# A Mamba layer inside a four-layer trunk: 64-row state tiles, softplus without a reciprocal, two groups projected from unnormed rows, two blocks of the last projection side by side

## The chip, the cores and the metric

The kernel runs on one core of a Trainium2 chip, in one launch. The metric is the device time of a run in microseconds (us). The kernel before took 1758.85, 1759.35 and 1761.85 us in three runs; the median is 1759.35 us.

## The reference

One inference step of four layers: an RG-LRU block, a Mamba-2 block (SSD), an RWKV-7 block and another RG-LRU block, each followed by a squared-ReLU MLP. 256 prompt tokens and 64 sample tokens (8 sequences of 8) go through the same weights, in float32. The change touches the Mamba-2 block alone:

```python
z, xbc, dt = split(rmsnorm(x, w) @ w_in, [2048, 2048 + 4096])
xbc = silu(causal_conv(xbc))                    # width 4, per channel
xs, B, C = split(xbc)                           # 8 groups: 256 x, 128 B, 128 C channels each
dt = softplus(dt + dt_bias)                     # 32 heads, 4 in a group
acs = cumsum(dt * A)                            # in a chunk (128 tokens) or a sample sequence (8)
y = (C B^T * exp(acs_i - acs_j) * mask) (dt * xs) + (C * exp(acs)) s_start
s_fin = s_start * exp(acs_end) + sum_j exp(acs_end - acs_j) dt_j x_j B_j^T   # new state
yg = (y + d_skip * xs) * silu(z)
yg = yg * rsqrt(mean over the group's 256 channels of yg^2)
x  = x + (yg * norm_w) @ w_out
```

Each of the 8 sample sequences has its own 128 x 256 state in every group, and all eight new ones are outputs.

## The kernel before

Features lie on the 128 partitions and the 320 tokens along them. Weights stream from one array in 512 KB chunks; each becomes a rounded half `whi` (an ACT copy, L494) and the rest `wlo` (a DVE subtraction, L495), in three buffers each. The activations are split likewise (`xh`, `xl`), and a product is three matmuls (L498 to L500): high by high, high by low, low by high. A chunk is 24 matmuls of 128x128 weights on 320 columns, called mains below.

The Mamba block (339 to 668 us of the profiled run) begins with the norm's factor `rs` per token. The inputs `xh`, `xl` hold at first the rows without that factor, so that projections start before it is known. `steps` computes dt for all heads on 32 partitions: softplus through `log1p_tail`, a scan `acs`, transposes (L926). `project(g)` computes a group's x half, its B and C and its z (two chunks each), and for each pair of results a convolution (ACT L849, DVE L851). Group 0 is projected from the unnormed rows, and `scaled` (L944, DVE) multiplies each result by `rs` into the tile `zs`, from which ACT copies it (L964, L965). Then `renorm` (L647, DVE; the split on ACT and DVE) makes the normed rows, and groups 1 to 7 use those; ACT copies their results straight from PSUM.

`ssd(g)` transposes x and B (L998), forms C B^T, the decays and masks (`em`), the old states' part (L1040), then the y products (L1072 to L1080), `yg`, and the group's norm (`nacc`, matmuls L595 and L611 to L613, `nrs`), whose result is split into `ygh`, `ygl`. For the new sample states ACT makes eight copies of B, each masked to one sequence (`bx`, L1060). 16 matmuls of 128x128 weights on 256 columns (L1101, L1102: x high, x low) go in four blocks into the bank `st_ps`, and DVE adds each block to the scaled old states (L1103; the scaling is L1095).

`weave` interleaves the parts of `ssd(g)` with those of `project(g + 1)`: the first number in its tuples says in how many parts a generator is stepped. The program so written goes to a list scheduler, which orders each engine's instructions by priority and readiness; the order on an engine is thus not the order in the text. After group 3, and at the end, `wout` multiplies four groups' `ygh`, `ygl` by the out-projection, four blocks of two chunks each. The last `wout` also fills PE while group 7 goes through its norm: the first half of each of its blocks (`ygh` of groups 4 and 5, then 6) doesn't need group 7.

Of the kernel before, what the change touches and what calls it, by code (L numbers as in the profile page):

```python
# [41 lines left out]
def _constants():  # L42
# [11 lines left out]
    m[64:, 384:448] = (js[:, None] // TS == js[None, :] // TS) & (js[:, None] <= js[None, :])  # L54
    b["cbmask"] = m
    bm = np.zeros((P, NB))
    bm[js, js // TS] = 1.0
    bm[64 + js, js // TS] = 1.0
    b["bmask"] = bm
# [76 lines left out]
def _weight_chunks(a):  # L136
# [23 lines left out]
    def layer_b():  # L160
# [10 lines left out]
        for mc in range(4):  # L171
            blk(wo, 1, mc)
# [245 lines left out]
def tile_hybrid_trunk(ctx: ExitStack, tc: tile.TileContext, wall, wlora, xt, wdt_d, s0_d, k0_d,  # L418
# [414 lines left out]
    def log1p_tail(pool, e, u, shape):  # L833

        d = pool.tile(shape, F32, name="lpd")
        m = pool.tile(shape, F32, name="lpm")
        ln = pool.tile(shape, F32, name="lpl")
        V.tensor_scalar(d, u, -1.0, None, op0=ALU.add)
        V.tensor_scalar(m, d, 0.0, None, op0=ALU.is_equal)
        S.activation(ln, u, AF.Ln)  # L840
        V.tensor_tensor(ln, ln, m, op=ALU.add)
        V.tensor_tensor(ln, ln, e, op=ALU.mult)
        V.tensor_tensor(d, d, m, op=ALU.add)
        V.reciprocal(d, d)
        V.tensor_tensor(ln, ln, d, op=ALU.mult)
        return ln
# [7 lines left out]
    def mixer_b(prep, nxt):  # L854
        with ExitStack() as st:
# [17 lines left out]
            def steps(ip):  # L873
# [41 lines left out]
                for q, a in enumerate((acs, dt, de, ea)):  # L915
                    V.tensor_copy(dup[:, q].rearrange("p (a t) -> p a t", a=2),
                                  a[:, TP:].unsqueeze(1).to_broadcast([NH, 2, NS]))
# [18 lines left out]
            def wout(prep2):  # L936
                for mc in range(4):
# [3 lines left out]

            def scaled(out, pt):

                V.tensor_tensor(out, pt[:, :, :N], b2(prep.rs), op=ALU.mult)  # L944

            def project(g, res):
# [3 lines left out]
                xsm = bp.tile([P, 4, 2, NS], F32, name="xsm")  # L950
# [5 lines left out]
                for half in range(2):  # L956
# [17 lines left out]
                for a in range(2):  # L974
                    S.activation(xsm[:, :, a].rearrange("p n (b t) -> p n b t", b=NB), smp(cv), AF.Copy)
# [4 lines left out]
                if g == 0:  # L980
                    scaled(zs, pt)
# [4 lines left out]
            def ssd(g, xbc, xsm, zs):  # L986
                bt = xbc[:, 2]
                ct = xbc[:, 3]

                xdt = ap.tile([P, 3, 4, 64], F32, name="xdt")  # L990
# [3 lines left out]
                for c in range(3):  # L994
                    pq = aux_ps()
                    for j in range(3):
                        src = xbc[:, j, c * P:(c + 1) * P] if c < 2 else xsm[:, j].rearrange("p a t -> p (a t)")
# [17 lines left out]
                T.matmul(pc[:, 384:448], xsm[:, 2].rearrange("p a t -> p (a t)"), xsm[:, 3, 0], start=True, stop=True)  # L1015
# [22 lines left out]
                for q in range(2):  # L1038
                    for j in range(4):
                        T.matmul(po[32 * j:32 * j + 32, 256 * q:256 * q + 256],  # L1040
                                 xsm[:, 3, 0, 32 * q:32 * q + 32], s0[:, 4 * q + j], start=True, stop=True)
# [16 lines left out]
                bx = ap.tile([P, NB, P], F32R, name="bx")  # L1058
                for b in range(NB):
# [5 lines left out]
                for m in range(2):  # L1065
# [15 lines left out]
                    for src, r in ((xbc[:, m, :TP], slice(0, TP)), (xsm[:, m, 0], slice(TP, N))):  # L1081
                        V.scalar_tensor_tensor(yg[:, m, r], src, vb("d")[:, 2 * g + m:2 * g + m + 1],
                                               py[:, r], op0=ALU.mult, op1=ALU.add)
# [768 lines left out]
```

## Time and profile before

| | |
|---|---|
| median of three runs | 1759.35 us |
| profiled execution, its own time | 1755.34 us |
| its span | 1753.3 us |
| PE, DVE, ACT busy | 1693.4, 1150.3, 978.0 us |
| granted TensorE clock, mean | 0.989 |
| Mamba block in the span | 339 to 668 us |

A duration of a matmul row is longer than its share of PE, since matmuls are pipelined: what one costs is the distance to the next row's start. "xN" on a row stands for N like instructions in a run. Idle time stands in brackets with what ended it. In the stretches a number in brackets counts instructions, and PEclk is the granted clock as a share of 2.4 GHz.

### The profile page before, as it was taken

To read this page: it belongs to the slowest core of one execution; us is meant where nothing else is said; L and a number is where in the kernel's file an instruction comes from. 1 tells how busy PE (TensorE), PEld (TensorE's weight loads), DVE (VectorE), ACT (ScalarE), POOL (GpSimd) and SP (SyncE) were. 2 spreads that over 40 slices of the span, in tenths; PEclk is the share of its full clock that TensorE was granted. 3 is DMA by queue.
4 is the path that set the end of the run, shared out by engine and by line. 5 is a ranking of instruction groups with operands and counts; after the bars stand their busy time and mean duration, and the time that the engine had idled before them with its cause. 6 is when DMAs were issued, how large, how long until landed. Compare 5 with 4: busy or idle time off the path is not lost.

```text
span 1753.3 us, 35969 instructions
## 1 busy us (share of the span) xinstructions
PE 1693.4 (97%) x15018; PEld 1635.1 (93%) x15018; DVE 1150.3 (66%) x1964; ACT 978.0 (56%) x1608; POOL 17.7 (1%) x36
## 2 busy tenths in 40 slices
PE   8999999989999999999999989899999999999997
PEld 7999999979999989999998977789999999999997
DVE  7975544499978976565467577786554469755444
ACT  7854443378857855553338566655543368554432
POOL 0000000000000000000000000000000000000000
PEclk9999999999999989999999999999999999999999
DMA  5444454545665534545434302134444444454452
GB/s 185 144 137 156 146 154 146 201 134 171 216 200 168 195 125 142 152 136 181 146 116 129 113 21 73 46 120 134 154 146 153 148 134 147 136 153 147 150 151 90
DMA packets 69746, 249.77 MB, mean 142 GB/s; under 512 B 9072, under 2 KB 11536, under 8 KB 67536
## 3 DMA queue, kind: packets, MB, share of 16 engines
q1 hardware_dynamic: 65040, 225.29, 41.5%
q0 software_dynamic: 2960, 18.89, 2.7%
q10 hardware_dynamic: 1584, 3.29, 0.5%
q8 instruction: 118, 1.93, 0.4%
q14 instruction: 44, 0.36, 0.1%
HBM read 233.52 MB, written 13.92 MB: 141 GB/s over the span
## 4 chain that ended last, share of the span: by engine, by line
PE 88%; DVE 7%; ACT 2%; issue 2%; DMA 1%; DVEq 0%; ACTq 0%
PE main_ps L498 22%; PE main_ps L500 22%; PE main_ps L499 22%; PE ps_b L1377 6%; PE aux_ps L499 2%; PE aux_ps L498 2%; PE aux_ps L500 2%; DVE wlo L495 1%; PE aux_ps L768 1%; DVE xc L792 1%; ACT whi L494 1%; PE ps_b L498 1%; PE ps_b L499 1%; PE ps_b L500 1%; PE ps_iu L1377 1%
## 5 line engine op out<-in xcount | busy, mean ns | idle before, releaser
L494 ACT ACTIVATE whi<-wraw 128x1024 fp32r<-128x1024 f32 x398 | 420.9, 1059 | 608.3 <-PE main_ps L499 512.4
L495 DVE TENSOR_TENSOR wlo<-wraw,whi 128x1024 fp32r<-128x1024 f32 x398 | 486.2, 1223 | 368.9 <-ACT whi L494 359.9
L498 PE MATMUL main_ps<-xh,whi 128*128 128x320 f32 x1664 | 521.4, 313 | 16.1 <-ACT whi L494 7.8
L499 PE MATMUL main_ps<-xl,whi 128*128 128x320 f32 x1664 | 518.8, 312 | 0.0
L500 PE MATMUL main_ps<-xh,wlo 128*128 128x320 f32 x1664 | 516.4, 310 | 0.9 <-DVE wlo L495 0.9
L498 PEld LDWEIGHTS main_ps<-xh,whi 128*128 128x128 f32 x1664 | 314.4, 189 | 18.4 <-ACT whi L494 8.0
L499 PEld LDWEIGHTS main_ps<-xl,whi 128*128 128x128 f32 x1664 | 314.3, 189 | 2.1 <-issue 0.4
L500 PEld LDWEIGHTS main_ps<-xh,wlo 128*128 128x128 f32 x1664 | 314.3, 189 | 2.0 <-DVE wlo L495 1.4
L500 PE MATMUL main_ps<-hh,wlo 128*128 128x320 f32 x768 | 237.2, 309 | 0.9 <-DVE wlo L495 0.9
L498 PE MATMUL main_ps<-hh,whi 128*128 128x320 f32 x768 | 237.0, 309 | 0.5 <-ACT whi L494 0.5
L499 PE MATMUL main_ps<-hl,whi 128*128 128x320 f32 x768 | 236.9, 309 | 0.0
L500 PEld LDWEIGHTS main_ps<-hh,wlo 128*128 128x128 f32 x768 | 144.0, 187 | 1.4 <-DVE wlo L495 1.4
L498 PEld LDWEIGHTS main_ps<-hh,whi 128*128 128x128 f32 x768 | 144.0, 187 | 0.8 <-ACT whi L494 0.8
L499 PEld LDWEIGHTS main_ps<-hl,whi 128*128 128x128 f32 x768 | 144.0, 187 | 0.0
L678 DVE SCALAR_TENSOR_TENSOR fr<-main_ps,nrs 128x640 f32<-128x640 f32 x64 | 52.7, 824 | 78.5 <-PE main_ps L500 78.5
L498 PE MATMUL aux_ps<-hh,whi 128*128 128x320 f32 x256 | 79.0, 309 | 0.0
L500 PE MATMUL aux_ps<-hh,wlo 128*128 128x320 f32 x256 | 79.0, 309 | 0.0
L499 PE MATMUL aux_ps<-hl,whi 128*128 128x320 f32 x256 | 79.0, 309 | 0.0
L495 DVE TENSOR_TENSOR hl<-fh,hh 128x640 fp32r<-128x640 f32 x64 | 52.8, 825 | 13.1 <-ACT hh L494 13.1
L851 DVE SCALAR_TENSOR_TENSOR cv<-sxb,k_b,cv 128x344 f32<-128x344 f32 x96 | 51.6, 569 | 0.8 <-ACT cv L849 0.8
L680 ACT ACTIVATE fh<-fr 128x640 f32<-128x640 f32 x64 | 47.3, 739 | 7.3 <-DVE fr L678 7.3
L662 DVE TENSOR_TENSOR x<-x,main_ps 128x320 f32<-128x320 f32 x56 | 24.8, 483 | 36.9 <-PE main_ps L500 36.9
(446 smaller groups left out, 2828.2 us busy)
## 6 DMA issues: line engine op xcount, KB each, us to landing
wraw<-in_wall SPq DMA_DIRECT2D x405, 512.0 KB, 3.7
ss<-in_s POOLq DMA_DIRECT2D x8, 1024.0 KB, 6.8
o_ssm_s<-ss POOLq DMA_DIRECT2D x8, 1024.0 KB, 4.3
acb<-acs_d SPq DMA_DIRECT2D x8, 640.0 KB, 3.9
wx<-in_k SPq DMA_DIRECT2D x8, 256.0 KB, 3.7
o_wkv_s<-wx SPq DMA_DIRECT2D x8, 256.0 KB, 2.7
o_ssm_p<-sp_o POOLq DMA_DIRECT2D x8, 128.0 KB, 4.3
wraw<-in_wlora SPq DMA_DIRECT2D x2, 512.0 KB, 3.7
```

Source lines behind the costliest of these rows:

```text
L494: S.activation(hi, src, AF.Copy)
L495: V.tensor_tensor(lo, src, hi.bitcast(F32), op=ALU.subtract)
L498: T.matmul(out, wh, ah, start=start, stop=False)
L499: T.matmul(out, wh, al, start=False, stop=False)
L500: T.matmul(out, wl, ah, start=False, stop=stop)
L662: ins = V.tensor_tensor(x[:, i], x[:, i], half(pt, m)[:, :N], op=ALU.add)
L678: V.scalar_tensor_tensor(r, pt[:, :, :N], 0.0, b2(prep.rs), op0=ALU.max, op1=ALU.mult)
L680: S.activation(h, r, AF.Square)
L768: T.matmul(pt[:, :NCV], w4[:, h % 4, s], xc[:, h, :NCV], start=True, stop=True)
L792: V.tensor_tensor_scan(xc[:, h, :NCV], ra[:, h], ix[:, h], 0.0, op0=ALU.mult, op1=ALU.add)
L851: V.scalar_tensor_tensor(out, src[:, k:k + NCV], w[k], out, op0=ALU.mult, op1=ALU.add)
L1377: return lambda *a, **k: tc.keep_in_program_order(fn(*a, **k))
```

## The change

1. `log1p_tail` forms ln(u) and then exp(-ln u) on ACT in place of the reciprocal on DVE; three DVE operations are left of seven.
2. The sample tokens of x, B and C are laid out so that partitions 0 to 63 hold sequences 0 to 3 (twice: high and low part) and 64 to 127 sequences 4 to 7. Four masked copies `bx` serve where eight did, each matmul of the state update has 64 rows, and the two halves go into two banks, `st_ps` and `nrm_ps` (the norm's). The text writes a low-half and a high-half matmul in turn.
3. Groups 0 and 1 are projected from the unnormed rows. DVE multiplies by `rs` straight into the convolution's input; ACT's copies go. `renorm` moves behind the weave of group 0 with group 1's projection, at high priority.
4. The last `wout` takes its first two blocks together (`chunk_mm2`: for each half of the inputs both blocks' chunks), the other two as before. The chunks lie in the weight array in that order.
5. `weave` steps `ssd` in 20 parts, not 26.

```diff
             if g == 4:
                 for mc in range(4):
                     blk(wo, 0, mc)
-        for mc in range(4):
+        out.append(np.stack([_wblk(wo, 1, j).reshape(P, 2, 1024) for j in range(2)], 2))
+        for mc in (2, 3):
             blk(wo, 1, mc)
...
         m = pool.tile(shape, F32, name="lpm")
         ln = pool.tile(shape, F32, name="lpl")
-        V.tensor_scalar(d, u, -1.0, None, op0=ALU.add)
-        V.tensor_scalar(m, d, 0.0, None, op0=ALU.is_equal)
         S.activation(ln, u, AF.Ln)
-        V.tensor_tensor(ln, ln, m, op=ALU.add)
-        V.tensor_tensor(ln, ln, e, op=ALU.mult)
-        V.tensor_tensor(d, d, m, op=ALU.add)
-        V.reciprocal(d, d)
-        V.tensor_tensor(ln, ln, d, op=ALU.mult)
+        S.activation(m, ln, AF.Exp, scale=-1.0)
+        V.scalar_tensor_tensor(d, u, -1.0, e, op0=ALU.add, op1=ALU.subtract)
+        V.tensor_tensor(d, d, m, op=ALU.mult)
+        V.tensor_tensor(ln, ln, d, op=ALU.subtract)
         return ln
...
             def wout(prep2):
-                for mc in range(4):
+                if prep2 is not None:
+                    pts = (main_ps(), main_ps())
+                    chunk_mm2(pts, ygh, ygl)
+                    for mc in range(2):
+                        add_out(pts[mc], mc, prep2)
+                for mc in range(0 if prep2 is None else 2, 4):
                     pt = main_ps()
                     chunk_mm(pt, ygh, ygl)
                     add_out(pt, mc, prep2)
 
-            def scaled(out, pt):
...
                     for _ in chunk_steps(pt, prep.h, prep.l):
                         yield
                     i = 2 * half
-                    if g == 0:
-                        scaled(zs, pt)
-                        pt = zs
-                    S.activation(pr[:, i:i + 2], pt[:, :, :TP], AF.Copy)
-                    S.activation(sa[:, i:i + 2], pt[:, :, TP:N].rearrange("p n (b t) -> p n b t", b=NB), AF.Copy)
+                    ps = pt[:, :, TP:N].rearrange("p n (b t) -> p n b t", b=NB)
+                    if g < 2:
+                        rs = prep.rs
+                        V.tensor_tensor(pr[:, i:i + 2], pt[:, :, :TP],
+                                        rs[:, :TP].unsqueeze(1).to_broadcast([P, 2, TP]), op=ALU.mult)
+                        V.tensor_tensor(sa[:, i:i + 2], ps, rs[:, TP:].rearrange("p (b t) -> p b t", b=NB)
+                                        .unsqueeze(1).to_broadcast([P, 2, NB, TS]), op=ALU.mult)
+                    else:
+                        S.activation(pr[:, i:i + 2], pt[:, :, :TP], AF.Copy)
+                        S.activation(sa[:, i:i + 2], ps, AF.Copy)
...
-                if g == 0:
-                    scaled(zs, pt)
+                if g < 2:
+                    V.tensor_tensor(zs, pt[:, :, :N], b2(prep.rs), op=ALU.mult)
                     pt = zs
...
                         S.activation(bhl, pq[:, 256:384], AF.Copy)
-                        V.tensor_tensor(bhl[:64], pq[:64, 256:384], bhl[:64].bitcast(F32), op=ALU.subtract)
+                        for r in (slice(0, 32), slice(64, 96)):
+                            V.tensor_tensor(bhl[r], pq[r, 256:384], bhl[r].bitcast(F32), op=ALU.subtract)
...
-                bx = ap.tile([P, NB, P], F32R, name="bx")
-                for b in range(NB):
+                bx = ap.tile([P, NB // 2, P], F32R, name="bx")
+                for b in range(NB // 2):
                     S.activation(bx[:, b], bhl.bitcast(F32), AF.Copy, scale=vb("bmask")[:, b:b + 1])
...
-                for b2_ in range(0, NB, 2):
-                    pn = side_ps("st_ps")
+                for b in range(0, NB // 2, 2):
+                    pn = [side_ps(t) for t in ("st_ps", "nrm_ps")]
                     for j in range(2):
-                        o = pn[:, 256 * j:256 * (j + 1)]
-                        T.matmul(o, bx[:, b2_ + j], xeh, start=True, stop=False)
-                        T.matmul(o, bx[:, b2_ + j], xel, start=False, stop=True)
-                    V.tensor_tensor(s0[:, b2_:b2_ + 2], s0[:, b2_:b2_ + 2],
-                                    pn.rearrange("p (b q) -> p b q", b=2), op=ALU.add)
+                        for i, xe in enumerate((xeh, xel)):
+                            for q, r in enumerate(HEADS):
+                                T.matmul(pn[q][:, 256 * j:256 * (j + 1)], bx[r, b + j], xe[r], start=i == 0, stop=i == 1)
+                    for q in range(2):
+                        s = s0[:, 4 * q + b:4 * q + b + 2]
+                        V.tensor_tensor(s, s, pn[q].rearrange("p (b q) -> p b q", b=2), op=ALU.add)
                     yield
                 nc.gpsimd.dma_start(o_ssm_s[g], s0.rearrange("p b q -> p (b q)"))
...
             weave((project(0, cur), 1, 0, 1))
-            with tc.high_priority(100):
-                prep.renorm(bp)
             for g in range(G):
                 last, cur = cur, []
-                parts = [(ssd(g, *last), 26, 0, 1)]
+                parts = [(ssd(g, *last), 20, 0, 1)]
                 if g + 1 < G:
                     parts.append((project(g + 1, cur), 11, 0.2, 1.2))
                 weave(*parts)
+                if g == 0:
+                    with tc.high_priority(100):
+                        prep.renorm(bp)
                 if g == 3:
                     wout(None)
```

The masks, `dup` and the transposes' sources follow the new layout; the constants have 1766 columns, not 1770. Lines are 3 or 4 lower up to `wout`, and a few higher behind it.

How the scheduler places this is seen at three places. On PE, behind group 2's y products (`bx` the masked B, `xeh`, `xel` x high and low, `main_ps` projections of the next group), before, a block of the state update:

```order
L611 MATMUL nrm_ps<-k_cm,nrr 128x128
L612 MATMUL nrm_ps<-k_cm,nrr 128x128
L613 MATMUL nrm_ps<-k_cm,nrr 128x64
L1101 MATMUL st_ps<-xeh,bx 128x256
L1102 MATMUL st_ps<-xel,bx 128x256
...
L499 MATMUL main_ps<-xl,whi 128x320
```

and after, where these matmuls have 64 rows:

```order
L1020 MATMUL aux_ps<-xsm 128x64
L1055 MATMUL st_ps<-xde,btk 128x256
L1108 MATMUL nrm_ps<-xeh,bx 128x256
L1108 MATMUL nrm_ps<-xel,bx 128x256
...
L497 MATMUL main_ps<-xh,whi 128x320
L498 MATMUL main_ps<-xl,whi 128x320
```

In both pieces "..." stands for the same two rows once more. The four matmuls of one half stand together, and those of the other half stand elsewhere: they don't alternate as written. Blocks of four with other work on both sides are the rule in all groups. Counted over the whole Mamba block, an instruction on PE has another tile of the array (128 rows by 128 columns, 64 by 128, 128 by 64, 32 by 128) than the one before it 28 times before and 83 times after, the old states' products (128 by 32) left aside.

On ACT, between the decays of one group and the convolution's Silu of the next (`nrt`, `nrr`, `nrs` the group norm, `zs` the Silu of z, `cv` that of the convolution), before:

```order
L601 ACTIVATE nrr<-nrt 128x6
...
L1031 ACTIVATE em<-em 128x1792
L615 ACTIVATE nrs<-nrm_ps 128x320
L973 ACT_TABLE_LOAD
L973 ACTIVATE cv<-cv 128x4x344
```

and after:

```order
L986 ACT_TABLE_LOAD
L986 ACTIVATE zs<-main_ps 128x640
L597 ACT_TABLE_LOAD
L597 ACTIVATE nrt<-nrm_ps,eps 128x6
L975 ACT_TABLE_LOAD
L975 ACTIVATE cv<-cv 128x4x344
L600 ACT_TABLE_LOAD
L600 ACTIVATE nrr<-nrt 128x6
```

The norm's Ln and Exp now stand between Silus, and each change of function set has a load of its own; over the whole program ACT has 61 loads, before 42.

On PE, behind the y products of group 7 (the last row of each piece is the first main of the out-projection that needs group 7), before:

```order
L1080 MATMUL aux_ps<-em,xdt 64x128 x2
L1102 MATMUL st_ps<-xel,bx 128x256
L1101 MATMUL st_ps<-xeh,bx 128x256
...
L498 MATMUL main_ps<-ygh,whi 128x320
L499 MATMUL main_ps<-ygl,whi 128x320
L500 MATMUL main_ps<-ygh,wlo 128x320
...
L595 MATMUL nrm_ps<-k_cm,nacc 128x2 x3
...
L498 MATMUL main_ps<-ygh,whi 128x320 x2
```

and after:

```order
L1086 MATMUL aux_ps<-em,xdt 64x128 x2
L1108 MATMUL st_ps<-xel,bx 128x256
L1108 MATMUL st_ps<-xeh,bx 128x256
...
L594 MATMUL nrm_ps<-k_cm,nacc 128x2 x3
L610 MATMUL nrm_ps<-k_cm,nrr 128x128
...
L497 MATMUL main_ps<-ygh,whi 128x320 x2
```

Before, 12 mains stand between the y products and the norm's matmuls; after, none do. Between group 6's y products and group 7's transposes (`aux_ps<-k_cm,cv`) stand 96 mains and 8 state matmuls after, 61 mains and 16 state matmuls before; up to the last row shown both have 108 mains.

Two more places can be told in a sentence. At the start of the block PE reaches the transposes of `acs` and `dt` (L922 after) behind 71 mains, before behind 99. In group 0 and 1 the 16 split instructions of `renorm` and its 8 products now stand between the convolutions of group 1 and those of group 2.

## Rows read from the trace of the kernel before

**Rows 1.** The page's part 1, first line: busy time, share, instructions.
```profile
PE 1693.4 (97%) x15018; PEld 1635.1 (93%) x15018; DVE 1150.3 (66%) x1964; ACT 978.0 (56%) x1608; POOL 17.7 (1%) x36
```

**Rows 2.** Stretches, core 0: length, busy (instructions) of each engine, PEclk, DMA share, GB/s.
```profile
348.15:398.40 50.25, 41.82 (x299) 38.66 (x297) 46.42 (x90) 36.75 (x72) 0.55 (x1) 0.93 0.44 139
549.40:580.10 30.70, 30.70 (x250) 29.01 (x248) 28.15 (x54) 26.42 (x53) 1.61 (x3) 1.00 0.61 209
```

**Rows 3.** Timeline of PE at its stalls: start, duration, instruction, [idle before, releaser].
```profile
359.25 0.39 PE L498 MATMUL main_ps<-xh,whi 128*128 128x320 f32 x1 [1.62 <-DVE zs L944]
...
361.86 0.24 PE L926 MATMUL aux_ps<-k_cm,acs 32*128 32x32 f32 x1 [1.20 <-DVE acs L899]
...
375.53 0.60 PE L498 MATMUL main_ps<-xh,whi 128*128 128x320 f32 x1 [5.62 <-DVE zs L944]
```

**Rows 4.** Stretches, PE alone: length, busy (instructions), PEclk, DMA share, GB/s.
```profile
376.00:380.00 4.00, 4.00 (x17) 0.50 0.65 215
380.00:384.00 4.00, 4.00 (x26) 0.87 0.80 296
```

**Rows 5.** Timeline of DVE in the softplus: start, duration, instruction.
```profile
353.55 0.48 DVE L841 TENSOR_TENSOR lpl<-lpl,lpm 32x320 f32<-32x320 f32 x1
...
354.77 2.13 DVE L844 RECIPROCAL lpd<-lpd 32x320 f32<-32x320 f32 x1
...
358.30 0.80 DVE L944 TENSOR_TENSOR zs<-main_ps,nrs 128x640 f32<-128x640 f32 x1
```

**Rows 6.** Tile unorm: operation, duration ns min/median/max, first and last start.
```profile
L647 DVE SCALAR_TENSOR_TENSOR unorm<-x,k_cm,nrs x8: 531/540/546, 349.3 to 371.7; 128x320 f32<-128x320 f32 x8
L495 DVE TENSOR_TENSOR xl<-unorm,xh x8: 483/484/494, 367.4 to 373.0; 128x320 fp32r<-128x320 f32 x8
```

**Rows 7.** Tiles ss and bx: operation, duration ns min/median/max, first and last start.
```profile
L1103 DVE TENSOR_TENSOR ss<-ss,st_ps x32: 674/680/690, 402.8 to 644.0; 128x512 f32<-128x512 f32 x32
...
L1060 ACT ACTIVATE bx<-bhl,k_b x64: 385/390/399, 391.2 to 631.8; 128x128 fp32r<-128x128 f32 x64
```

**Rows 8.** Timeline of PE, layer C: a 128-row matmul, then pairs on 64 rows.
```profile
941.82 0.31 PE L499 MATMUL main_ps<-xbl,whi 128*128 128x320 f32 x1
941.97 0.31 PE L500 MATMUL main_ps<-xbh,wlo 128*128 128x320 f32 x1
942.21 0.42 PE L498 MATMUL main_ps<-loh,whi 64*128 64x320 f32 x2
942.46 0.31 PE L499 MATMUL main_ps<-lol,whi 64*128 64x320 f32 x2
942.60 0.32 PE L500 MATMUL main_ps<-loh,wlo 64*128 64x320 f32 x2
```

**Rows 9.** Timeline of PE, end of the y products, first state matmuls.
```profile
610.38 0.42 PE L1080 MATMUL aux_ps<-em,xdt 128*64 128x128 f32 x4
610.73 0.39 PE L1101 MATMUL st_ps<-xeh,bx 128*128 128x256 f32 x1
610.95 0.28 PE L1102 MATMUL st_ps<-xel,bx 128*128 128x256 f32 x1
611.07 0.27 PE L1101 MATMUL st_ps<-xeh,bx 128*128 128x256 f32 x1
```

**Rows 10.** Timeline of ACT around a table load: start, duration, instruction.
```profile
619.52 0.42 ACT L615 ACTIVATE nrs<-nrm_ps 128x320 f32<-128x320 f32 x1
619.97 1.28 ACT L973 ACT_TABLE_LOAD   x1
621.26 1.36 ACT L973 ACTIVATE cv<-cv 128x1376 f32<-128x1376 f32 x1
```

**Rows 11.** Timeline of PE, last group: transposes, y products, idle at the end.
```profile
622.97 0.82 PE L998 MATMUL aux_ps<-k_cm,cv 128*128 128x128 f32 x6
...
638.98 0.83 PE L595 MATMUL nrm_ps<-k_cm,nacc 128*128 128x2 f32 x6 [1.31 <-DVE nacc L572]
...
644.95 0.90 PE L498 MATMUL main_ps<-ygh,whi 128*128 128x320 f32 x2 [1.39 <-ACT ygh L494]
```

More of the change, by code (lines that the diff above doesn't have):

```diff
@@ L53, in _constants @@
     js = np.arange(NS)
-    m[64:, 384:448] = (js[:, None] // TS == js[None, :] // TS) & (js[:, None] <= js[None, :])
+    jr = 32 * h + r % 32
+    m[:, 384:448] = (s[:, None] >= 32) & (jr[:, None] // TS == js[None, :] // TS) & (jr[:, None] <= js[None, :])
     b["cbmask"] = m
[L56 to L59, printed above, removed]
+    b["bmask"] = r[:, None] % 32 // TS == np.arange(NB // 2)[None, :]
     t = np.arange(32)
@@ L940, in wout @@
                     add_out(pt, mc, prep2)
-            def scaled(out, pt):
-                V.tensor_tensor(out, pt[:, :, :N], b2(prep.rs), op=ALU.mult)
             def project(g, res):
@@ L949, in project @@
                 cv = bp.tile([P, 4, NXB], F32, name="cv")
-                xsm = bp.tile([P, 4, 2, NS], F32, name="xsm")
+                xsm = bp.tile([P, 4, 2, 2, 32], F32, name="xsm")
                 zs = bp.tile([P, 2, N], F32, name="zs")
@@ L974, in project @@
                 for a in range(2):
-                    S.activation(xsm[:, :, a].rearrange("p n (b t) -> p n b t", b=NB), smp(cv), AF.Copy)
+                    S.activation(xsm[:, :, :, a].rearrange("p n q (b t) -> p n q b t", t=TS),
+                                 smp(cv).rearrange("p n (q b) t -> p n q b t", q=2), AF.Copy)
                 yield
@@ L996, in ssd @@
                     for j in range(3):
-                        src = xbc[:, j, c * P:(c + 1) * P] if c < 2 else xsm[:, j].rearrange("p a t -> p (a t)")
+                        src = xbc[:, j, c * P:(c + 1) * P] if c < 2 else xsm[:, j].rearrange("p q a t -> p (q a t)")
                         T.transpose(pq[:, j * P:(j + 1) * P], src, ident)
@@ L1014, in ssd @@
                 T.matmul(pc[:, 256:384], bt[:, 128:256], ct[:, 128:256], start=True, stop=True)
-                T.matmul(pc[:, 384:448], xsm[:, 2].rearrange("p a t -> p (a t)"), xsm[:, 3, 0], start=True, stop=True)
+                T.matmul(pc[:, 384:448].rearrange("p (q t) -> p q t", q=2), xsm[:, 2].rearrange("p q a t -> p (q a t)"),
+                         xsm[:, 3, :, 0], start=True, stop=True)
                 cbm = ap.tile([P, 448], F32, name="cbm")
@@ L1040, in ssd @@
                         T.matmul(po[32 * j:32 * j + 32, 256 * q:256 * q + 256],
-                                 xsm[:, 3, 0, 32 * q:32 * q + 32], s0[:, 4 * q + j], start=True, stop=True)
+                                 xsm[:, 3, q, 0], s0[:, 4 * q + j], start=True, stop=True)
                 yo = ap.tile([P, 2, 4, 64], F32, name="yo")
@@ L1080, in ssd @@
                                 T.matmul(o[:, 128:256], xdt[:, 1, h], em[:, h, 256:384], start=False, stop=True)
-                    for src, r in ((xbc[:, m, :TP], slice(0, TP)), (xsm[:, m, 0], slice(TP, N))):
-                        V.scalar_tensor_tensor(yg[:, m, r], src, vb("d")[:, 2 * g + m:2 * g + m + 1],
-                                               py[:, r], op0=ALU.mult, op1=ALU.add)
+                    for src, r in ((xbc[:, m, :TP], slice(0, TP)), (xsm[:, m, :, 0], slice(TP, N))):
+                        o, i = (t if r.start == 0 else t.rearrange("p (q t) -> p q t", q=2) for t in (yg[:, m, r], py[:, r]))
+                        V.scalar_tensor_tensor(o, src, vb("d")[:, 2 * g + m:2 * g + m + 1], i, op0=ALU.mult, op1=ALU.add)
                     V.tensor_tensor(yg[:, m], yg[:, m], zs[:, m], op=ALU.mult)
```

4 lines of the change are left out of this document (2 added, 2 removed).

## The prediction

> **What bounds the kernel now.** I read the busy times first [rows 1]: PE 1693.4 of 1753.3 us, DVE 1150.3, ACT 978.0. PE is the bound on the whole, but a share says nothing of one stage, so the stretches come next [rows 2]. A middle group of the Mamba block takes 30.70 us and PE is busy in all of it; DVE has 2.55 us left, ACT 4.28. At the block's start it is otherwise: of 50.25 us PE works 41.82, at 0.93 of the clock, and DVE works 46.42. There both are short: PE waits for DVE, and DVE has only 3.83 us of slack. PE's timeline [rows 3] tells for what: 1.62 us for a scaled copy queued on DVE behind the softplus, 1.20 us for the scan `acs`, 5.62 us for group 0's last scaled copy, which stood on DVE behind the renorm. After that longest wait the clock is at its lower level [rows 4]: 17 and then 26 mains start in 8 us. At the upper level mains start 0.147 us apart in the mean (0.15 and 0.14 in [rows 8]), so 54 would have fitted; 11.4 x 0.147 = 1.7 us are lost. The third place is the end of the block [rows 11]: 1.31 and 1.39 us of idle in the chain from group 7's y products to the split `ygh`.
>
> The sum is made on the profiled execution (1755.34 us, 2.0 more than its span), and then moved to the median, which lies 4.0 us higher.
>
> **1. The start: -1.8 us (-6.4 to 0).** On PE's side: the wait of 5.62 us goes, because group 1 no longer needs the renorm, and with it the slow 1.7 us. Of the first two waits, together 2.8 us, one remains: PE reaches the transposes 28 mains (4.1 us) earlier, near 354.9 us (361.86 less the two waits and 4.1). DVE's softplus falls from 2.13 plus six operations of up to 0.48 [rows 5] to three of 0.48, so `acs` comes some 3.2 us earlier, near 358: a wait of about 3 us. PE alone would thus gain 7.3 - 0.3 = 7.0.
>
> DVE doesn't allow it. Its work in this stretch hardly shrinks: softplus -3.2; per projected result pair the sum is now a 128x512 product (0.68 [rows 7]), one of 128x128 (an estimate of 0.3 from the same row) and for z 0.8, in two groups 5.5, against three scaled copies of 0.80 before [rows 5], so +3.1; one more `bhl` subtraction +0.3. The net is zero. DVE's slack was 3.83 us, and with that of the following group (2.55) 6.4 bounds the gain. The renorm's DVE part, 8 x (0.54 + 0.48) = 8.2 us [rows 6], now comes between groups 1 and 2, and PE, ahead by then, meets it there: the wait is moved, and DVE sits under it. Queues on DVE never close up wholly; I take a little over a quarter of the slack, 1.8.
>
> **2. The clock at the start: +0.8 us (0 to 1.7).** The one wait of 3 us is longer than those of 1.62 and 1.20 us and shorter than that of 5.62 us behind which the lower level is seen [rows 3, 4]. The trace doesn't say on which side it lies; I take half of the 1.7.
>
> **3. The state update on 64 rows: +8.2 us (+4.1 to +10.7).** The number of matmuls is the same, 16 in a group on 256 columns, 0.115 us apart [rows 9]. Two halves would have to be side by side in the array to save anything, and in the order they don't alternate: four of one half, then something else, then four of the other. So nothing is saved. But every such run puts another tile shape on the array, and that has a price in this trace. In layer C [rows 8] the step from the last 128-row matmul to the first 64-row one is 0.24 us in place of 0.147, and the next is 0.25: 0.09 + 0.10. On the way back to 128 by 128, behind the y products [rows 9], the first state matmul takes 0.22 to the next in place of 0.12: 0.10 again, with the step before it not to be read there. I take 0.195 us for a change of shape, either way. The order counts 28 before and 83 after: 55 more, 7 in a group. In groups 1 to 6 PE never waits [rows 2], so they are paid in full: 42 x 0.195 = 8.2. In groups 0 and 7 they fall into stretches in which PE waits anyway; with those the bound is 55 x 0.195 = 10.7. Half a price (one of the two steps hidden) gives 4.1. The masked copies, four fewer of 0.39 in a group on ACT [rows 7], free an engine that isn't the bound.
>
> The Trainium skill speaks for this part of the change: "TensorEngine Tiling (Array Packing)", section "Theoretical Speedup", gives a contraction of up to 64 rows up to twice the speed. That holds for tiles that run side by side, as the pairs of rows 8 do (two in 0.146 us); by it the term would be that of the first rival below.
>
> **4. Waits in the middle groups: +0.8 us (0 to 2).** ACT gets 19 more table loads of 1.28 us [rows 10], 2.4 in a group or 3.0 us, and loses 4 x 0.39 = 1.6: of its 4.28 us of slack 2.8 stay. But some loads stand in the norm's own chain (Ln, load, Silu, load, Exp), so `nrs` comes later by two of them, 2.6 us, and DVE's scaling of the old states can stand ahead of `nacc`. PE has projections to run meanwhile; I take 0.8 in all.
>
> Here a rule speaks against the change: the Trainium skill, "ScalarE: Activation LUTs", section "What ACT_TABLE_LOAD costs", adds a drain to each load, 2.66 us in all. In this trace a load begins 0.03 us after the instruction before it ends and the next begins 0.01 us after the load [rows 10]; no drain is seen, so the measurement decides. By the rule ACT would want 6.4 us where 5.9 are free, and the term would be some 3 us larger.
>
> **5. The end: +3.8 us (1.9 to 6.4).** From the end of group 6's y products (610.73) to group 7's transposes (622.97) PE ran 61 mains, 16 state matmuls and the norm's, 12.2 us [rows 9, 11]. Now 96 mains stand there: +35 x 0.147 = 5.1, 8 state matmuls fewer -0.9, three or so changes of shape with fewer norm matmuls -0.4: 3.8 later. From those transposes on it is a chain (decays, y, `yg`, norm, `ygh`), 22.0 us until the out-projection goes on at 644.95; the mains that lay beside it before now lie ahead of it, and the same 108 are done by then. So the chain's later start is paid in full. Low end: half of it, since the splits of weights for those mains stood on ACT and DVE within the chain and now stand ahead of it. High end: two table loads of 1.28 more in the chain. The side-by-side blocks change nothing else: same chunks, same matmuls.
>
> **Sum.** -1.8 + 0.8 + 8.2 + 0.8 + 3.8 = +11.8: the profiled run 1767.1, the median 1771.2, so 1771.
>
> **Rivals.**
> - *The halves run side by side (faster).* If the 64-row runs of both banks overlap, each group saves half of its 16 x 0.115, in all 7.4 us, and no change of shape is felt. The sum is then -1.8 + 0.8 - 7.4 + 0.8 + 3.8 = -3.8, the median 1755.6; with the whole slack won at the start 1751. For it: pairs do run so in layer C [rows 8]. Against it: there they alternate, here they don't. It decides once both halves of a block stand next to each other in most groups. The Trainium skill has the rule, in "TensorE: Matmul & The Clock Gate", section "The mechanism": tiles in different row groups overlap. Chance 0.15.
> - *The prices cancel (no change).* DVE's slack is won at the start (-6.0 with the clock kept), half of each change of shape is hidden (+4.1), the end takes its low value (+1.9), the middle nothing: 0.0, median 1759. For it: PE's waits at the start are the largest in the block [rows 3]. Against it: DVE at 46.42 of 50.25 [rows 2]. Chance 0.14.
> - *More late than that.* Nothing won at the start, the slow clock there, all 55 changes paid, loads in every chain: 0 + 1.7 + 10.7 + 2 + 6.4 = +20.8, median 1780. For it: the loads stand in the norm's chain. Chance 0.15.
>
> **How the numbers follow.** The forecast has 0.56. About 0.2%, 3.5 us, is what a measurement of this kernel can tell from no change. Below that on the fast side lies the first rival and a little of the second: 0.17. Within it 0.15, mostly the second. Slower 0.68. The forecast's own range, by its terms' ends taken together by halves, is 1763 to 1778; the range for 8 in 10 reaches to the first rival below and to the third above, 1755 to 1780.
>
> **What would show it.** Part 3 right: state rows with 64*128 in runs of four, a first step of 0.22 to 0.25 in each, and middle groups of about 32.1 us in place of 30.7. Wrong: pairs with one step for two, or groups as long as before. Part 1 right: no wait of 5.6 us before group 1, but PE waits for `xl` behind group 0's y products, and these end only a little earlier for group 1 than before. Wrong: group 1's y products 5 us or more earlier. Part 5 right: from the end of group 6's y products to the main that ends the wait on `ygh` 38 us, before 34.2. The whole is wrong if the middle groups keep their 30.7, for then the rest sums to about +3.6.

## The result: slower by 1.6%, more than forecast

The changed kernel takes 1787.65 us (median of four runs, 1783.44 to 1791.28); the kernel before, in the runs beside it, 1759.1. The ratio is 1.0159, with a 95% interval from 1.0142 to 1.0176; the medians differ by 28.5 us. The forecast was +11.8, its range ended at 1780.

Where it went is read from the profiled executions (spans 1785.5 and 1753.3 us) with the y products of the eight groups as landmarks. The block starts with PE's first main of it, y0 is the start of group 0's y products, and "end" is the main behind the block that waits for its `whi` (694.44 us after, 668.38 before).

| | before | after | difference |
|---|---|---|---|
| block starts at | 338.7 | 342.3 | +3.6 |
| its start to y0 | 57.5 | 51.4 | -6.1 |
| y0 to y1 | 30.7 | 41.6 | +10.9 |
| y1 to y6 | 181.6 | 191.4 | +9.8 |
| y6 to end | 59.8 | 67.7 | +7.9 |
| behind the block | 1084.9 | 1091.0 | +6.1 |

The block itself loses 22.4 us, and 3.6 are lost ahead of it. The change thus doesn't touch the Mamba block alone, as the reference's section says: the first layer, an RG-LRU block, forms its coefficients with `log1p_tail` too. There the Exp has a table load of its own, the norm's `nrs` comes at 27.58 us in place of 24.25, and PE waits for `xb`, which is scaled by it:

```profile
19.12 1.28 ACT L838 ACT_TABLE_LOAD   x1
27.58 0.42 ACT L614 ACTIVATE nrs<-nrm_ps 128x320 f32<-128x320 f32 x1
30.01 0.39 PE L497 MATMUL main_ps<-xh,whi 128*128 128x320 f32 x1 [2.61 <-DVE xb L756]
```

Among the sixteen kernels of this study all seven with the new softplus have this wait, and their block starts at 342.3 to 345.1 us; the nine with the old one don't have it, and theirs starts at 338.4 to 339.6.

The last row lies in layers that the change reaches only through `log1p_tail`. Over the sixteen profiles it goes from 1078.1 to 1091.0 us, in ones with the old softplus (1078.1 to 1086.2) and the new (1082.2 to 1091.0), and the second RG-LRU block shows no such wait. I count it as spread and not as the change's; no run separates the two.

### The profile page after: what moved, and what is told of

Read it like the earlier page. It is cut to its first block, busy times and chain, and to the rows that moved or that the text cites. A ratio compares the mean times of both kernels' runs of the same rounds, so it can differ in the third digit from the quotient of the medians.

```text
span 1785.5 us, 35946 instructions
## 1 busy us (share of the span) xinstructions
PE 1709.8 (96%) x15018; PEld 1641.6 (92%) x15018; DVE 1153.0 (65%) x1967; ACT 992.8 (56%) x1590; POOL 17.7 (1%) x36
## 4 chain that ended last, share of the span: by engine, by line
PE 86%; DVE 8%; ACT 2%; issue 2%; DMA 1%; DVEq 0%; ACTq 0%; POOLq 0%
PE main_ps L497 22%; PE main_ps L498 22%; PE main_ps L499 22%; PE ps_b L1385 6%; PE aux_ps L498 2%; PE aux_ps L497 2%; PE aux_ps L499 2%; DVE wlo L494 2%; PE aux_ps L767 1%; DVE xc L791 1%; PE nrm_ps L1108 1%; PE ps_iu L1385 1%; PE ps_b L497 1%; ACT whi L493 1%; PE ps_b L498 1%
## 5 line engine op out<-in xcount | busy, mean ns | idle before, releaser
L497 PE MATMUL main_ps<-xh,whi 128*128 128x320 f32 x1664 | 523.0, 314 | 11.5 <-ACT whi L493 7.9
L493 ACT ACTIVATE hh<-fh 128x640 fp32r<-128x640 f32 x64 | 47.4, 741 | 2.0
```

What stands on the lines that cost most here:

```text
L493: S.activation(hi, src, AF.Copy)
L497: T.matmul(out, wh, ah, start=start, stop=False)
```

## The profile after

Busy times, the page's first line:

```profile
PE 1709.8 (96%) x15018; PEld 1641.6 (92%) x15018; DVE 1153.0 (65%) x1967; ACT 992.8 (56%) x1590; POOL 17.7 (1%) x36
```

PE works 16.4 us more than in [rows 1] on as many matmuls, and the rest of the 32 us is waiting. PE's waits in and behind the block (waiting line, releaser, total us, times, longest):

```profile
PE st_ps L1108 <- DVE ss L1111: 5.3, 2, 2.7
PE aux_ps L922 <- DVE acs L895: 3.5, 1, 3.5
PE nrm_ps L610 <- DVE nrr L608: 2.3, 4, 1.3
PE main_ps L499 <- DVE wlo L494: 2.1, 2, 1.2
PE main_ps L498 <- DVE xl L494: 1.6, 1, 1.6
```

The 5.62 us of [rows 3] are gone, and its 1.62 and 1.20 are one wait of 3.5, as worked out. New are waits for `ss`, DVE's additions of the state blocks, and for `xl` and `wlo`. The stretches of the start and, last, from y2 to y3 (length; busy time of PE, PEld, DVE, ACT, POOL; PEclk; DMA share; GB/s):

```profile
345.00:393.70 48.70, 45.22 (x304) 42.03 (x302) 36.38 (x77) 30.28 (x55) 0.55 (x1) 0.96 0.55 191
393.70:411.00 17.30, 15.93 (x134) 14.81 (x133) 16.26 (x35) 14.64 (x31) 0.00 (x0) 1.00 0.32 100
411.00:420.00 9.00, 5.15 (x18) 3.75 (x19) 8.12 (x16) 4.54 (x7) 0.54 (x1) 0.66 0.08 31
420.00:437.50 17.50, 17.50 (x139) 15.78 (x138) 14.73 (x26) 10.51 (x21) 1.08 (x2) 0.88 0.70 235
467.32:499.11 31.79, 31.79 (x249) 29.19 (x248) 26.65 (x50) 28.98 (x52) 1.08 (x2) 1.00 0.50 166
```

The kernel before had, from the same 345 us to its own y0:

```profile
345.00:396.20 51.20, 42.77 (x280) 40.11 (x278) 44.22 (x89) 34.62 (x68) 0.55 (x1) 0.93 0.46 154
```

Here is the largest thing that the forecast missed. Up to y0 DVE has 12.3 us free after, where it had 7.0 before. Then, from 393.7 to 420, it is busy in 24.4 of 26.3 us while PE stops: in the 9 us from 411 PE starts 18 matmuls, at 0.66 of the clock. The work has moved from a place where PE waited anyway to one where DVE had none to spare. The renorm could not have used the free time before y0: it writes over the rows that group 1's mains still read, and its copies into `xh` (tile, count, duration in ns, first and last start) begin only here:

```profile
L493 ACT ACTIVATE xh<-unorm x8: 450/454/473, 397.7 to 414.5; 128x320 fp32r<-128x320 f32 x8
```

A middle group (last of the stretches after, [rows 2]) has 31.79 us in place of 30.70, PE busy throughout.

PE in such a group, one run of state matmuls (start, duration, instruction):

```profile
481.04 0.31 PE L497 MATMUL main_ps<-xh,whi 128*128 128x320 f32 x1
481.27 0.38 PE L1108 MATMUL st_ps<-xeh,bx 64*128 64x256 f32 x1
481.49 0.28 PE L1108 MATMUL st_ps<-xel,bx 64*128 64x256 f32 x1
...
481.73 0.27 PE L1108 MATMUL st_ps<-xel,bx 64*128 64x256 f32 x1
481.94 0.41 PE L498 MATMUL main_ps<-xl,whi 128*128 128x320 f32 x1
482.19 0.31 PE L499 MATMUL main_ps<-xh,wlo 128*128 128x320 f32 x1
```

The step from the last main to the first 64-row matmul is 0.23, the next 0.22; on the way back 0.21 and 0.25. Against 0.147 and 0.115 that is 0.08 to 0.1 each, as [rows 8, 9] had it. In the kernel before, the same work on 128 rows has no such step between two mains (0.15 in, 0.12 behind it):

```profile
621.91 0.31 PE L498 MATMUL main_ps<-ygh,whi 128*128 128x320 f32 x1
622.06 0.28 PE L1101 MATMUL st_ps<-xeh,bx 128*128 128x256 f32 x1
622.18 0.27 PE L1102 MATMUL st_ps<-xel,bx 128*128 128x256 f32 x1
```

ACT ahead of the last group's transposes:

```profile
639.96 1.28 ACT L597 ACT_TABLE_LOAD   x1
...
641.54 1.28 ACT L975 ACT_TABLE_LOAD   x1
...
644.21 1.28 ACT L600 ACT_TABLE_LOAD   x1
645.51 0.21 ACT L600 ACTIVATE nrr<-nrt 128x6 f32<-128x6 f32 x1
```

Three loads of 1.28 us in 6 us, and `nrr` of group 6's norm comes behind the convolution's Silu. The end of PE's chain, then DVE behind the last y products, after and before:

```profile
645.28 0.82 PE L1002 MATMUL aux_ps<-k_cm,cv 128*128 128x128 f32 x6
...
656.08 0.65 PE L1078 MATMUL aux_ps<-em,xdt 128*64 128x256 f32 x4 [0.36 <-DVE em L1038]
...
661.59 0.35 PE L1108 MATMUL st_ps<-xeh,bx 64*128 64x256 f32 x1 [2.57 <-DVE ss L1111]
...
663.44 1.44 PE L594 MATMUL nrm_ps<-k_cm,nacc 128*128 128x2 f32 x6 [1.14 <-DVE nacc L571]
...
670.20 0.58 PE L1108 MATMUL nrm_ps<-xeh,bx 64*128 64x256 f32 x1 [0.78 <-DVE ss L1111]
...
671.35 0.90 PE L497 MATMUL main_ps<-ygh,whi 128*128 128x320 f32 x2
```

```profile
657.00 2.28 DVE L1101 TENSOR_TENSOR ss<-ss,eend 128x2048 f32<-128x2048 f32 x1
659.20 0.47 DVE L1089 SCALAR_TENSOR_TENSOR yg<-cv,k_b,aux_ps 128x256 f32<-128x256 f32 x1
```

```profile
632.21 2.28 DVE L1095 TENSOR_TENSOR ss<-ss,eend 128x2048 f32<-128x2048 f32 x1
634.41 0.47 DVE L1082 SCALAR_TENSOR_TENSOR yg<-cv,k_b,aux_ps 128x256 f32<-128x256 f32 x1
```

From the transposes at 645.28 to the out-projection at 671.35 are 26.1 us, in [rows 11] 22.0. The scaling of the old states (2.28 us) stands on DVE ahead of the first `yg` in both kernels, so its place isn't what is new. The 4.1 us come in three pieces. The y products start 10.8 us behind the transposes, before 9.2: group 6's late norm and two of its state additions now stand on DVE ahead of `em`. The first `yg` comes 3.1 us behind them, before 2.2. From the norm's sums to the out-projection are 7.9 us, before 6.0: two state blocks that go into the norm's bank stand directly ahead of it and wait for `nrs` (0.53) and `ss` (0.78), while before PE waited there for `ygh` itself. From `yg` to the sums it is no longer than before (4.2, before 4.6), though PE waits 2.57 us there for a state block.

## The experiments

Lengths from each run's profile, in us; "ratio" is to the kernel before in runs beside it, with its 95% interval.

| run | ratio | block at | to y0 | y0-y1 | y1-y6 | y6-end |
|---|---|---|---|---|---|---|
| before | 1 | 338.7 | 57.5 | 30.7 | 181.6 | 59.8 |
| changed | 1.0159 (1.0142 to 1.0176) | 342.3 | 51.4 | 41.6 | 191.4 | 67.7 |
| b_soft | 1.0005 (0.9991 to 1.0019) | 345.1 | 52.9 | 30.7 | 181.8 | 58.5 |
| b_wout | 0.9993 (0.9979 to 1.0008) | 339.2 | 59.4 | 30.8 | 181.7 | 58.2 |
| b_grp | 1.0018 (1.0003 to 1.0033) | 338.9 | 55.5 | 40.1 | 181.7 | 59.7 |
| b_grp_np | 1.0027 (1.0012 to 1.0041) | 339.2 | 56.8 | 40.9 | 181.7 | 60.0 |
| b_all | 1.0034 (1.0021 to 1.0047) | 339.6 | 51.8 | 30.8 | 187.6 | 63.4 |
| b_five | 1.0035 (1.0014 to 1.0056) | 339.3 | 57.0 | 31.1 | 195.4 | 59.8 |
| b_20 | 1.0074 (1.0055 to 1.0093) | 338.4 | 59.2 | 31.0 | 187.9 | 64.0 |
| b_state | 1.009 (1.0075 to 1.0105) | 338.5 | 56.3 | 30.1 | 191.9 | 71.1 |
| b_pairs | 1.0054 (1.0035 to 1.0072) | 338.5 | 55.9 | 28.3 | 186.2 | 69.8 |
| a_nostate26 | 1.0044 (1.0031 to 1.0057) | 345.1 | 52.4 | 39.9 | 181.7 | 56.7 |
| a_nostate | 1.0066 (1.005 to 1.0081) | 342.5 | 51.8 | 35.8 | 188.5 | 65.7 |
| a_nogrp | 1.0118 (1.0094 to 1.0142) | 343.3 | 53.7 | 31.8 | 192.9 | 67.5 |
| a_26 | 1.0137 (1.0113 to 1.016) | 345.1 | 49.0 | 38.8 | 191.9 | 71.1 |
| a_pairs | 1.0135 (1.0117 to 1.0154) | 343.7 | 50.6 | 37.6 | 191.5 | 69.2 |

In b_state, b_pairs and a_26 more mains stand behind y6 (276 to 283 in place of 240), some 6 us of the last column, and fewer ahead of y1. One profile stands for a row: from the block's start to y0 are 57.5 us in one and 59.4 and 59.2 in two others that don't differ from it there. Totals are taken from the ratios.

### Parts alone: b_soft, b_wout

b_soft has the new `log1p_tail` alone, b_wout the last `wout` alone, each with that piece of the diff above.

> The kernel before with part 1 alone (softplus without the reciprocal). My working gave acs 3.2 us earlier on DVE, but PE waits for group 0's scaled copies behind it all the same: 0 to -2 us, about 1757; the two first waits at the start fall together from 2.8 to 0 to 1 us unless PE comes there earlier.

> The kernel before with part 4 alone (first two blocks of the last out-projection side by side). My prediction held that this changes nothing by itself: within 1.5 us of the kernel before, from group 6's y products to the end of the block 59.8 us as there. Rival: the second chunk's split holds up PE while group 7 goes through its chain, +2 to +4 us.

Neither moves the time. In b_soft PE waits 2.90 us for `acs` in one piece: it comes there earlier, as the forecast had it. Counted from the block's start, y1 comes 4.7 us earlier than before; but the block starts 6.4 us later, behind the wait for `xb` in the first layer, with the clock down behind it (0.66 from 29 to 34 us, before 1.00). The zero is thus the sum of a gain and a loss, and the forecast saw the gain alone.

### Part 3: b_grp, b_grp_np, a_nogrp, b_all, b_five

```diff
 b_grp: part 3's pieces of the diff on the kernel before
 b_grp_np:
-                    with tc.high_priority(100):
-                        prep.renorm(bp)
+                    prep.renorm(bp)
 b_all: no renorm
-                    if g < 2:
+                    if g < G:
 b_five:
-                if g == 0:
+                if g == 3:
-                    if g < 2:
+                    if g < 5:
 a_nogrp: part 3 taken back from the changed kernel
```

> The kernel before with part 3 alone (groups 0 and 1 from unnormed rows, renorm behind group 0's weave). Theory A (the moved renorm takes DVE from group 0's chain and starves PE between the y products of groups 0 and 1, as in the changed kernel, where that stretch grew by 10.9 us): +6 to +9 us, about 1766, with the stall for xl there and the clock down behind it. Theory B (what stalls PE there is the 64-row state blocks, which wait in PE's order for DVE's additions): -2 to -5 us, about 1755, since the 5.6 us wait is gone.

The total, 0.2% more, lies between the two theories. The wait of 5.6 us is gone, and y0 to y1 takes 40.1 us without any 64-row tile, so the blocks of part 2 don't make it: A holds for the place, though what PE waits for is `ss` and not `xl`. PE:

```profile
415.98 0.58 PE L1106 MATMUL st_ps<-xeh,bx 128*128 128x256 f32 x1 [4.90 <-DVE ss L1108]
```

and DVE between the two additions of which the second releases PE:

```profile
409.60 0.68 DVE L1108 TENSOR_TENSOR ss<-ss,st_ps 128x512 f32<-128x512 f32 x1
...
412.05 0.54 DVE L647 SCALAR_TENSOR_TENSOR unorm<-x,k_cm,nrs 128x320 f32<-128x320 f32 x1
...
413.46 0.48 DVE L495 TENSOR_TENSOR xl<-unorm,xh 128x320 fp32r<-128x320 f32 x1
...
415.24 0.68 DVE L1108 TENSOR_TENSOR ss<-ss,st_ps 128x512 f32<-128x512 f32 x1
```

```profile
416.00:424.00 8.00, 7.89 (x36) 7.59 (x37) 6.07 (x14) 2.75 (x6) 0.54 (x1) 0.60 0.62 222
```

Between the additions at 409.60 and 415.24 stand `ygl`, two of the renorm's products, three splits of its rows (L495) and three steps of group 1's convolution. PE idles 4.9 us, and the stretch behind it runs at 0.60 of the clock.

> The kernel before with part 3 alone, and renorm at ordinary priority: on DVE the state additions of group 0 now stand ahead of six of the eight splits. Theory A1 (DVE's capacity: 8.2 us of renorm no longer fit into PE's idle time, whatever their order): from group 0's y products to group 1's still 37 to 40 us, only the releaser changes (xl in place of ss), total as b_grp. Theory A2 (the order: PE's state blocks wait for additions that stand behind the renorm): 31 to 34 us there, total some 6 us under b_grp, about 1753.

With the additions first the stretch is 40.9 us and the total as in b_grp: the order is not what counts (A2 falls). PE's waits only change places (3.3 us for `ss`, 1.3 for the scaled z). That leaves DVE's room, as A1 has it, but not proven: the renorm also overwrites the rows in place, so it can't begin before group 1's last mains have read them, and no run gives it buffers of its own. Part of the loss is the lower clock behind the stall: a_nostate, which has part 3 too, takes 35.8 us there with the clock at 1.00 throughout.

> The changed kernel with part 3 undone (group 0 alone from unnormed rows, renorm ahead of group 0's weave). If the start's loss is part 3's (8.3 us in the trace up to group 1's y products), the stretch is 31 to 33 us and the total 7 to 9 us under the changed kernel. If the state blocks and loads make it, it stays at 38 to 41 us and the total changes by less than 2 us.

y0 to y1 falls to 31.8, and the ratio by 0.0041, some 7 us, as the first theory had it (the two intervals just touch). Part 3 costs about that much in the changed kernel; alone it costs 0.2%.

> The kernel before with part 3 carried to all eight groups: every group is projected from the unnormed rows and scaled on DVE, and there is no renorm. If the loss of part 3 is the renorm's 8.2 us of DVE work at a place where DVE has no room: from group 0's y products to group 1's 31 to 32 us (40.1 with part 3 as it is), PE's 5.6 us wait gone as well, and group 1's y products end 5 to 7 us earlier than before. The middle groups then have 2.8 us more DVE work each (28.2 -> 31.0 us in 30.7): 0 to 0.6 us longer each. Total -2 to -6 us, about 1754. If the scaled copies themselves crowd DVE: the stretch stays over 35 us.

```profile
345.00:391.40 46.40, 42.28 (x287) 39.98 (x286) 36.54 (x75) 30.50 (x56) 0.55 (x1) 0.96 0.49 176
391.40:422.10 30.70, 30.70 (x248) 28.97 (x247) 29.17 (x55) 24.67 (x48) 1.61 (x3) 1.00 0.54 190
```

Without the renorm y0 to y1 is 30.8 us, and y1 stands at 422.1, 4.9 us ahead of before in this profile. But groups 1 and 2 are some 1.6 us longer each (more than the 0 to 0.6 expected), group 3 with the out-projection 2.5, and y6 to the end 3.6, so the total is slower still. Groups 4 and 5 have the same scaled copies and take 30.7 and 30.9 us: the copies alone don't make a group longer, and what does in groups 1 to 3 is not shown.

> The kernel before with part 3 drawn out: groups 0 to 4 from unnormed rows, and renorm behind group 3's weave, where PE has 192 mains of the out-projection that need no normed rows. If the renorm's place is what costs: no stall for it anywhere; group 1's y products 5 us earlier than before, groups 1 to 3 as in b_all (some 1.6 us longer each from the scaled copies on DVE), groups 5 to 7 and the end as before: 0 to -2 us in all, against +6 for b_all. If scaled copies cost wherever they stand: +3 or more.

The renorm stalls PE under the out-projection as well, though 192 mains there don't need it: from group 3's y products to group 4's are 69.5 us, 8.0 more than in b_all. The longest wait is for the same thing as in b_grp:

```profile
513.13 0.58 PE L1106 MATMUL st_ps<-xeh,bx 128*128 128x256 f32 x1 [4.39 <-DVE ss L1108]
```

So the renorm costs at each of the two new places, and there are longer groups (1 and 2) where scaled copies stand. What it costs at the old place no run shows. Nor is y1 5 us earlier here: up to there this kernel differs from b_all only by four products of the renorm, yet y1 stands at 427.3, with the clock at 0.87 from 345 us to y0 where b_all had 0.96. The early start of b_all is one profile's and not repeated. This version beats neither b_grp nor the kernel before.

### Parts 2 and 5: b_state, b_20, a_nostate, a_nostate26, a_26

```diff
 b_20:
-                parts = [(ssd(g, *last), 26, 0, 1)]
+                parts = [(ssd(g, *last), 20, 0, 1)]
 b_state: part 2's pieces on the kernel before, 26 parts
 a_nostate: part 2 taken back from the changed kernel; a_nostate26: and 26 parts
 a_26: the changed kernel with 26 parts
```

> The kernel before with part 2 alone (sample states on two 64-row tiles; ssd still in 26 parts, 42 table loads). Theory A (each change of tile shape on PE costs 0.195 us, and the order has some 50 more of them): middle groups 30.7 -> 32.0 us, +9 us in all, about 1768. Theory B (the changes of shape are cheap; the loss comes from the 19 table loads that ssd in 20 parts brings): under +3 us, 1759 to 1762.

More than A expected, with no table load added. Its middle groups have 16 changes of shape and not 11: mains stand between the two halves of the y products too. The five intervals from y1 to y6 have 80 changes, before 20: 60 x 0.195 = 11.7 us against +10.3 in the table (with six mains fewer, 0.9 us).

> The changed kernel with part 2 undone (state update on 128 rows, eight bx; ssd in 20 parts, 60 table loads). Theory A (shape changes): middle groups back to about 30.8 us, -9 to -12 us, about 1777; the rest is parts 3 and 4. Theory B (table loads): hardly faster than the changed kernel, 1784 to 1788.

Theory A holds for the total (0.9% under the changed kernel, 16 us, more than expected), but the middle groups don't go back to 30.8. Something else lengthens them:

> The kernel before with part 5 alone (ssd in 20 parts; 56 loads). If the loads cost: middle groups 31.0 to 32.0 us with short waits for ACT's btk and ygh in them, the end 3 to 5 us longer, total +5 to +9 us. If not, within 2 us of the kernel before.

> The kernel before with parts 1, 3 and 4, ssd in 26 parts: 44 loads (60 with ssd in 20 parts, which took 11 us more than the kernel before). If the loads of the 20 parts cost: as part 3 alone, +2 to +4 us, middle groups 30.7 us, and from group 6's y products to the end 59 to 60 us. If not: still +9 to +11.

Stepping `ssd` in 20 parts costs 0.7% by itself, 13 us and more than expected: 56 loads, waits for `btk`, `ygh` and `ygl`, 6 changes of shape in a group, +6.3 us in the middle and +4.2 at the end. a_nostate26 comes out between its two theories: middle groups of 30.7 us and a short end (56.7), but +0.4%, for the start's 39.9 and the late block are left. With parts 1, 3 and 4 the 20 parts add 0.2% (1.0066 against 1.0044), with everything 0.2% (1.0159 against 1.0137). In both pairs the intervals overlap. Beside the other parts the 20 parts thus cost less than alone; that their waits fall together with the others' is argued, not shown.

> The changed kernel with ssd stepped in 26 parts as before: 44 table loads in place of 61, 119 changes of tile shape in place of 87. If loads cost most at the end: the last group's transposes come 3 to 4 us earlier after group 6's y products and the total falls by 3 to 5 us, against some 32 x 0.2 = 6 us more for the shapes: about equal, within 3 us of the changed kernel. If the shapes have no price: 4 us under it.

The total is 0.2% (4 us) under the changed kernel, with overlapping intervals: it can't decide between the two. The profile says more. From y1 to y6 PE never waits, with 82 changes of shape, and the stretch is 10.3 us longer than before with eight mains fewer (1.2 us): 62 x 0.195 = 12.1 against 11.5.

### Side by side: a_pairs, b_pairs

```diff
-                            for q, r in enumerate(HEADS):
-                                T.matmul(pn[q][...], bx[r, b + j], xe[r], ...)
+                            for q, r in ((1, HEADS[1]), (0, HEADS[0])):
+                                ins = T.matmul(pn[q][...], bx[r, b + j], xe[r], ...)
+                                if (i, j, q) != (0, 0, 1):
+                                    tc.keep_in_program_order(ins)
```

> The changed kernel, with the matmuls of a state block held in one run of eight on PE that alternates the halves (nrm_ps, st_ps). If halves in turn run side by side and a change of shape costs 0.195 us: a run of 8 takes about 0.5 us and not 0.9, and a group has 4 changes fewer: -1.7 us a group, middle groups 30.3 to 30.6 us, -10 to -13 us in all, about 1776. If they don't run side by side, -0.8 a group, about 1781. If the shape has no price, no change: 1787.

PE in a_pairs, one run:

```profile
456.92 0.38 PE L1108 MATMUL nrm_ps<-xeh,bx 64*128 64x256 f32 x1
456.93 0.38 PE L1108 MATMUL st_ps<-xeh,bx 64*128 64x256 f32 x1
457.14 0.28 PE L1108 MATMUL nrm_ps<-xel,bx 64*128 64x256 f32 x1
457.15 0.28 PE L1108 MATMUL st_ps<-xel,bx 64*128 64x256 f32 x1
...
457.38 0.28 PE L1108 MATMUL nrm_ps<-xel,bx 64*128 64x256 f32 x1
457.38 0.28 PE L1108 MATMUL st_ps<-xel,bx 64*128 64x256 f32 x1
457.59 0.41 PE L497 MATMUL main_ps<-xh,whi 128*128 128x320 f32 x1
```

Two matmuls start within 0.01 us of each other: in turn, the halves do run side by side, 8 in 0.67 us with the way out. A group's 16 take 1.3 to 1.6 us; before they took 2.1, in the changed kernel 2.7. Yet y1 to y6 is as long as there, and the total falls by 0.2% (4 us, intervals overlapping) and not by 10 to 13 us. PE now waits 5.2 us from y1 to y6, where the changed kernel had 2.0, for ACT, which has 62 loads, and for the norm; behind the waits of the first out-projection the clock is at its lower level as well (0.69 in the 11 us from 515).

```profile
PE nrm_ps L610 <- DVE nrr L608: 2.1, 2, 1.4
PE main_ps L497 <- ACT zs L986: 1.7, 2, 1.5
PE aux_ps L1002 <- ACT cv L975: 0.8, 1, 0.8
```

> The kernel before with part 2 alone, ssd in 26 parts (42 loads), and the state blocks in runs of eight that alternate the halves. b_state took 15 us more than before with 16 changes of shape in a middle group and single halves. If pairs cost half and each change 0.195 us: state matmuls 1.35 in place of 2.65 us a group, some 4 to 6 changes fewer, so middle groups 2.0 to 2.4 us shorter than b_state's: 30.5 to 31.3 us, total +1 to +5 us against before. If the changes aren't the cause of b_state's loss: 1768 or more.

With 42 loads the matmuls' gain arrives: y1 to y6 186.2 us, 5.7 under b_state, and the ratio falls from 1.009 to 1.0054, which is still more than the 1 to 5 us expected. At 0.195 us each, the 12 to 14 changes of shape in a group (before 4) cost more than the 0.4 to 0.8 us that the pairs save against 128 rows.

No run beats the kernel before; b_wout and b_soft can't be told from it.

## Why the prediction was wrong in size

It forecast slower, for the reason that makes a large part of the loss (changes of shape), and fell short by 16.7 us of 28.5.

1. *The start (-1.8 forecast; +4.7 from the block's start to y1).* This is the step that failed: "the wait is moved, and DVE sits under it", with 0 as the worst end. I bounded the gain by DVE's slack over the whole start and took the renorm's 8.2 us as moved at no cost. Up to y0 the working held, and better than I took it: `acs` comes 3.7 us earlier behind the block's start (3.2 worked out), and y0 6.1 us earlier, near the bound of 6.4. But then y0 to y1 loses 10.9 us. Slack counts where it lies. After, DVE is free before y0, when the rows can't yet be overwritten because group 1's mains read them (the copies into `xh` start at 397.7); behind y0 DVE has group 0's norm and states, group 1's copies and convolutions, and the renorm at once. The rival "More late than that" had 0 here, and even that was too kind. That the renorm's new place costs is shown by b_grp, a_nogrp and b_all; how much of it is DVE's room and how much the overwriting in place stays open. In the total part 3 costs less than its profiles show (+0.2% alone, some 7 us of the changed kernel).
2. *Ahead of the block (no term; +3.6 measured).* The sum had nothing outside the Mamba block, and gave no reason for that. The new softplus makes PE wait 2.61 us in the first layer.
3. *The clock (+0.8).* Behind the wait for `acs` twelve mains start 0.267 us apart and not 0.147; with a step on either side 1.5 us are lost, near the upper end. That the clock falls again behind the stall at 411 I had not seen; it is part of point 1.
4. *Changes of shape (+8.2).* Right in price and place: y1 to y6 has 58 changes after and 20 before, 38 x 0.195 = 7.4 us of the +9.8. Most of the rest is idle time of PE around the first out-projection (1.20 for `wlo`, 0.64 for `nrr`).
5. *Waits in the middle (+0.8).* They are 2.0 us, the upper end. I judged the table loads by ACT's free time, which is left indeed (28.98 of 31.79 us busy). Of the 2.0 us 0.8 are for `nrr`, in the norm's chain; a_26, with 44 loads, has no wait from y1 to y6.
6. *The end (+3.8, measured +7.9).* The transposes of group 7 start 16.4 us behind the first state matmul after group 6's y products (628.90), before 12.2 [rows 9, 11]: +4.1, as worked out. What was wrong is the chain behind them, which I held at 22.0 us: it takes 26.1, so that the main that needs `ygh` comes 42.4 us behind group 6's y products and not 38. The pieces are in the section on the profile; that group 6's table loads start them is read from the order, not shown by a run.

## What to carry to other kernels

Slack on an engine is worth something only at the place where the moved work will stand: take the stretches on both sides of a new place one by one, and ask what each buffer still holds there. Small matmuls on a part of the array can save time only if the final order keeps the halves in turn and in long runs, since each change of shape cost 0.2 us of the whole PE queue here; even runs of eight lost in b_pairs. A helper that a change rewrites has other callers: price it at each of them. And the number of steps in an interleaving is a change of its own: read the table loads and the order of the chain after it.

## What was not expected of the hardware

Two matmuls on the two halves of the rows, with their own weights, start 0.00 to 0.01 us apart and end together, here with 256 columns as in [rows 8] with 320. A state block of 8 then costs 0.46 us from the first start to the last pair's, and about 0.4 us more for the two changes of shape around it. From its first start to the next main it takes 0.67 us, as long as a run of four on one half in the changed kernel (481.27 to 481.94).
